# A hybrid encoder step: residual kept transposed, output projection with standing weights, the norm's factor applied after the projections

## Chip, cores and metric

One NeuronCore of a Trainium2 chip runs the whole program. The metric is the device time of one execution in microseconds (us), as a median over runs. The engines are named PE (TensorE), DVE (VectorE), ACT (ScalarE), POOL (GpSimd) and SP (SyncE, here the queue of all DMAs).

## What is computed

Four layers (A, B, C, A) update 576 tokens (512 of a prompt, 64 of a sample) of width 1024. Each layer has one input projection that gives the mixer's inputs and a gate of width 1024, a mixer, and an output projection:

```python
def rmsnorm(x, g):
    y = x * lax.rsqrt(jnp.mean(x * x, axis=-1, keepdims=True) + 1e-6)
    return y * g

def mixer_a(xp, ...):                       # chunked attention, 8 heads of 128
    z = rmsnorm(x, norm_g) @ w_in           # 1024 -> 4096: q, k, v, gate
    q, k = rmsnorm(q, q_g), rmsnorm(k, k_g) # per head
    o = band_attend(q, k, v, ...)
    return (o * silu(gate)) @ w_out         # 1024 -> 1024
# mixer_b: window attention, 16 query and 4 key heads of 64
# mixer_c: latent attention; q through a normed 512-wide latent, k and v through a normed 256-wide one
for i in range(4):
    x = x + mixer[i](x)
```

Besides the new x, the new keys, values and latents are outputs.

## The kernel before

All projections are f32 in two parts: each operand is split into a high part (rounded to fp32r by ACT, `AF.Copy`) and a low part (the difference, by DVE or POOL), and a product is three matmuls: high x high, high x low, low x high. They add up in one PSUM accumulator over the 8 blocks of 128 inputs. PSUM has three accumulators `mm` (`ps_mm`), two for transposes (`ps_t`), two for scores and one for attention outputs.

Activations for a projection stand transposed in SBUF, inputs on the partitions: `xT` (tile `T`) for the input projections, `oT` for the output projection. In `mm_tok` (lines 154 to 175) a tile of 128 tokens of these is the standing operand and up to 512 weight columns move; the last 64 tokens have their high and low parts side by side as one standing tile of 128, so they take two matmuls (lines 168 and 169) and a fold of the two halves (lines 172 to 174). In `gates` (line 211) the weights stand and half of the tokens, 288 columns, move (lines 224 to 226); the gate's tanh form is then multiplied into the branch result `o`.

The residual x lives in DRAM between layers, tokens on the rows. At the end of a layer `split_o` (line 250) splits each of the 8 blocks of the branch result into `oT`, high part on ACT, low part on POOL in two pieces (512 and 64 columns). `oT` lies in memory that the layer's own tiles have given up, and the blocks are interleaved with the last gates by `mix`. Then x is loaded again (`load_x`, 5 token tiles) and `out_proj` (line 256) runs over two halves of the output columns, each over 5 token tiles; after a tile's second half its x is stored and `norm` (line 184) makes the next layer's `xT` from it: a sum of squares on ACT, the factor per token by a power on POOL (`rstd`, line 112), two scaled copies on DVE (line 193), eight transposes on PE (line 178, `tr`), and the split out of PSUM (lines 181 and 182).

Weights are loaded in pieces of 256 KB (`load_chunk`: 512 columns of one block, `load_packed`: 256 columns of two blocks) into 4 staging buffers `ws` and split into 8 pairs `wh`, `wl`. Program order is that of the code; a planner then orders each engine's instructions by expected readiness before the launch, so that accumulators of one pool can be worked on side by side, and each engine runs its list in that order.

Of the kernel before, what the change touches and what calls it, by code (L numbers as in the profile page):

```python
# [18 lines left out]
D = 1024  # L19
# [21 lines left out]
def encoder_step(ctx: ExitStack, tc: tile.TileContext, I, O):  # L41
# [58 lines left out]
    x = []  # L100
# [3 lines left out]
    def load_x(pool, src):  # L104
        x.clear()
        for t, (t0, tn) in enumerate(TT):
            xt = sb(D, f"x{t}", pool=pool)
            last = ld(xt[:tn], src[t0 : t0 + tn, :])
            x.append(xt)
        return last.ins  # L110
# [43 lines left out]
    def mm_tok(xT, nh, t0, tn, pieces, n, p=None, c0=0, w0=0):  # L154
        p = p or ps_mm()
        last = len(pieces) - 1
        out = p[:, c0 : c0 + n]
        ws = slice(w0, w0 + n)
        for i, (h, l) in enumerate(pieces):
            if tn == 128:  # L160
                xh = xT[:, i, t0 : t0 + tn]
                xl = xT[:, i, nh + DEC + t0 : nh + DEC + t0 + tn]
                PE.matmul(out, xh, h[:, ws], start=(i == 0), stop=False)  # L163
                PE.matmul(out, xh, l[:, ws], start=False, stop=False)  # L164
                PE.matmul(out, xl, h[:, ws], start=False, stop=(i == last))  # L165
# [6 lines left out]
        lo = sb(512, "lo", 1)[:64, :n]  # L172
# [11 lines left out]
    def norm(t, g, xT):  # L184
        t0, tn = TT[t]
        ss = sb(1, "nss", pool=tiny)[:tn]
        junk = sb(D, "sq", 2, dt=BF16)[:tn]
        S.activation(junk, x[t][:tn], AF.Square, accum_out=ss)
        r = rstd(ss, tn, 1, 1.0 / D)
        for hf in range(2):  # L190
            xs = rows_of(tn)
            cs = slice(hf * 512, hf * 512 + 512)
            V.scalar_tensor_tensor(out=xs[:tn], in0=x[t][:tn, cs], scalar=r, in1=g[:tn, cs], op0=ALU.mult, op1=ALU.mult)  # L193
            pt = v3(ps_t(), 128)
            for j in range(4):
                tr(pt[:, j, :], xs[:, j * 128 : j * 128 + 128])
            k0 = hf * 4
            l0 = lo_at(t0, TOK)
            hl_evac(xT[:, k0 : k0 + 4, t0 : t0 + tn], xT[:, k0 : k0 + 4, l0 : l0 + tn], pt[:, :, :tn])
            if tn == DEC:  # L200
                end = V.tensor_copy(xT[:, k0 : k0 + 4, 2 * TOK : WT], xT[:, k0 : k0 + 4, TOK : TOK + DEC].bitcast(F32))
        return end.ins if tn == DEC else None
# [8 lines left out]
    def gates(xT, w, c0, ogs, done=None):  # L211
        st = []

        def half(m, og, hf):
# [12 lines left out]
            th = sb(512, "sq", 2)[:, :HALF]  # L227
# [22 lines left out]
    def split_o(oT, b, src):  # L250
        S.activation(oT[:, b, :TOK], src, AF.Copy)  # L251
        for a, c in ((0, SEQ), (SEQ, TOK)):
            l0 = lo_at(a, TOK)
            G.tensor_tensor(out=oT[:, b, l0 : l0 + c - a], in0=src[:, a:c], in1=oT[:, b, a:c].bitcast(F32), op=ALU.subtract)  # L254

    def out_proj(w, oT, after):
        for nh in range(2):
            pieces = load_chunk(w, [(nh * 512, 512)])
            for t in range(len(TT)):
                t0, tn = TT[t]  # L260
                p = mm_tok(oT, TOK, t0, tn, pieces, 512)
                xs = x[t][:tn, nh * 512 : nh * 512 + 512]
                V.tensor_tensor(out=xs, in0=p, in1=xs, op=ALU.add)  # L263
                after(t, nh)
# [7 lines left out]
    def layer_a(li, xT, first=None):  # L272
        w = I["a_w_in"][li]
        with tc.tile_pool(name=f"la{li}", bufs=1, reuse_waits="tile") as lp:
# [4 lines left out]
            def v_units(pr, pieces=None):  # L279
                st = [pieces] if pieces else []  # L280

                def unit(ts, tn):
# [11 lines left out]
                    S.activation(vt[:tn, ts[0] : ts[0] + n, :], v3(p, 256), AF.Copy)  # L294
                    for t in ts:
# [4 lines left out]
            def qk_units(pr):  # L300
                st = []

                def unit(t, t0, tn):
# [10 lines left out]
                    r = rstd(ss, tn, 4, 1.0 / 128)  # L314
# [131 lines left out]
    def layer_b(xT):  # L446
        w = I["b_w_in"][0]
        with tc.tile_pool(name="lb", bufs=1, reuse_waits="tile") as lp:
# [25 lines left out]
            for t, (t0, tn) in enumerate(TT):  # L474
# [27 lines left out]
            def q_units(g):  # L502
                w_ = []

                def unit(t, t0, tn):
# [9 lines left out]
                    r = rstd(ss, tn, 4, 1.0 / 64)  # L515
# [143 lines left out]
    def layer_c(xT):  # L659
        w = I["c_w_in"][0]  # L660
        with tc.tile_pool(name="lc", bufs=1, reuse_waits="tile") as lp:
# [52 lines left out]
            for t, (t0, tn) in enumerate(TT):  # L714
# [4 lines left out]
                r = rstd(ss, tn, 1, 1.0 / 512)  # L719
# [9 lines left out]
            for t, (t0, tn) in enumerate(TT):  # L729
# [5 lines left out]
                r = rstd(ss, tn, 2, [(0, 1, 1.0 / 256), (1, 2, 1.0 / 32)])  # L735
# [176 lines left out]
    def gain(pool, nm, i):  # L912
        g = sb(D, "gain", pool=pool)
        ld(g, I[f"{nm}_norm"][i : i + 1].to_broadcast([128, D]))
        return g

    layers = [("a", 0), ("b", 0), ("c", 0), ("a", 1)]
# [3 lines left out]
    with tc.tile_pool(name="xp0", bufs=1) as xp:  # L921
        for t, (t0, tn) in enumerate(TT):
            xt = sb(D, f"x{t}", pool=xp)
            ld(xt[:tn], I["x"][t0 : t0 + tn, :])
            x.append(xt)
            if t == 0:
                ld(ident, I["ident"])
                nxt_gain = gain(xp, "a", 0)
            if t < 4:
                src = I["a_w_in"][0][256 * t : 256 * t + 256, 2048:2304].rearrange("(a p) c -> p a c", p=128)  # L930
                h, l = load_w([src], 512, 256)
                first += [(h[:, 256 * i : 256 * i + 256], l[:, 256 * i : 256 * i + 256]) for i in range(2)]
            end = norm(t, nxt_gain, xT)
# [3 lines left out]
        with tc.issue_after(end):  # L937
            for a, b, f in ((0, 2, 128 ** -0.5), (2, 3, 64 ** -0.5), (8, 32, -1.0)):
# [3 lines left out]
    x_src = I["x"]  # L942
    for i, (kind, li) in enumerate(layers):
# [6 lines left out]
        x_new = dp.tile([TOK, D], F32, tag=f"xd{i}", name=f"xd{i}") if i < 3 else O["y"]  # L950
        nxt = {}

        def after(t, nh):
            t0, tn = TT[t]
            if i == 3:
                ld(x_new[t0 : t0 + tn, nh * 512 : nh * 512 + 512], x[t][:tn, nh * 512 : nh * 512 + 512])
            elif nh == 1:
                if "xT" not in nxt:
                    nxt["xT"] = big_xT()
                ld(x_new[t0 : t0 + tn], x[t][:tn])  # L960
                norm(t, nxt_gain, nxt["xT"])

        with tc.tile_pool(name=f"op{i}", bufs=1, reuse_waits="tile") as op:
            oT = v3(sb(KD * WT, "oT", dt=F32R, pool=op), WT)
# [3 lines left out]

            units = tail(put)
            after_gate = {"a": (6, 7), "b": (6, 7), "c": CT}[kind]  # L970
            mix([lambda b=b: put(b) for b in range(KD) if b not in after_gate], units)
            late[0] = load_x(op, x_src)
            if i < 3:
                nxt_gain = gain(op, *layers[i + 1])
            out_proj(I[f"{kind}_w_out"][li], oT, after)
# [5 lines left out]
    "y": (TOK, D),  # L981
# [94 lines left out]
```

## Time and profile before

| | |
|---|---|
| median of 3 runs | 1273.11 us (1271.35 to 1273.27) |
| the profiled execution | 1273.74 us, span of its instructions 1272.0 us |
| mean granted PE clock | 0.998 |
| PE, weight loads, DVE, ACT, POOL busy | 98%, 86%, 57%, 51%, 30% |
| DMA | 127.18 MB, mean 100 GB/s |

The span runs from the first to the last instruction of the program; launch and end lie around it. Matmuls are pipelined: the recorded duration of one overlaps the next, so the distance between starts, not the duration, is what a matmul costs in a stream.

### The profile page before, as it was taken

The numbers are of one execution on the slowest core, as the hardware profiler recorded it, in microseconds if no ns is written. First come the engines' busy times: TensorE is split into PE (matmuls) and PEld (weight loads), VectorE is DVE, ScalarE is ACT, GpSimd is POOL, SyncE is SP. The second block draws the span as 40 slices with busy tenths as digits, with TensorE's granted clock in tenths as the row PEclk, the third lists the DMA queues.
The fourth block names the chain that finished last, engine by engine and source line by source line (L and its number), as shares of the span: only waits on it lengthen the run. The fifth ranks groups of instructions, "written<-read, shape, count | busy, mean of one in ns | idle before, by whom it ended". The sixth has DMA issues, their size and how long they took to land.

```text
span 1272.0 us, 22132 instructions
## 1 busy us (share of the span) xinstructions
PE 1242.3 (98%) x7927; PEld 1090.7 (86%) x7927; DVE 719.3 (57%) x1979; ACT 647.7 (51%) x1645; POOL 383.1 (30%) x492
## 2 busy tenths in 40 slices
PE   5999999999999999999999999999999999999998
PEld 5889898998889999778998887876788898989986
DVE  5365535433668887526577767675264655354432
ACT  5345444553446776614466767676243454445431
POOL 5321212114035451331275444541311212121150
PEclk9999999999999999999999999999999999999999
DMA  7235241442446231344131111112343352414322
GB/s 210 83 96 152 77 140 53 141 128 76 154 126 215 74 87 51 113 121 137 57 101 53 53 30 34 34 51 69 98 157 99 94 159 73 144 43 138 129 80 70
DMA packets 99613, 127.18 MB, mean 100 GB/s; under 512 B 11184, under 2 KB 77648, under 8 KB 99440
## 3 DMA queue, kind: packets, MB, share of 16 engines
q1 hardware_dynamic: 99504, 125.77, 32.5%
q8 instruction: 62, 1.02, 0.3%
q14 instruction: 47, 0.39, 0.1%
HBM read 105.81 MB, written 24.26 MB: 102 GB/s over the span
## 4 chain that ended last, share of the span: by engine, by line
PE 94%; DVE 2%; ACT 2%; DMA 1%; issue 0%; POOL 0%; SPq 0%; DVEq 0%; POOLq 0%; ACTq 0%
PE mm L163 16%; PE mm L165 16%; PE mm L164 16%; PE t L178 9%; PE mm L224 5%; PE mm L225 5%; PE mm L226 5%; PE mm L168 4%; PE mm L169 4%; PE o L383 3%; PE s L858 3%; PE o L868 2%; PE s L375 2%; PE o L595 1%; PE s L562 1%; PE s L563 1%
## 5 line engine op out<-in xcount | busy, mean ns | idle before, releaser
L116 POOL TENSOR_TENSOR nv<-nv,mhalf 128x4 f32<-128x4 f32 (+7 forms) x147 | 150.9, 1031 | 470.8 <-DVE nv L115 446.7
L163 PE MATMUL mm<-wh,T 128*128 128x256 f32 (+2 forms) x736 | 246.3, 338 | 3.6 <-ACT T L181 2.4
L165 PE MATMUL mm<-wh,T 128*128 128x256 f32 (+2 forms) x736 | 246.4, 336 | 0.0
L164 PE MATMUL mm<-wl,T 128*128 128x256 f32 (+2 forms) x736 | 243.3, 335 | 0.0
L120 ACT ACTIVATE wh<-ws 128x512 fp32r<-128x512 f32 (+2 forms) x288 | 169.2, 614 | 111.9 <-PE mm L168 74.9
L121 DVE TENSOR_TENSOR wl<-ws,wh 128x512 fp32r<-128x512 f32 (+2 forms) x252 | 170.8, 698 | 48.2 <-ACT wh L120 44.7
L224 PE MATMUL mm<-T,wh 128*128 128x288 f32 x512 | 155.5, 304 | 0.1
L163 PEld LDWEIGHTS mm<-wh,T 128*128 128x128 f32 x736 | 140.8, 192 | 15.2 <-ACT T L181 2.8
L225 PE MATMUL mm<-T,wh 128*128 128x288 f32 x512 | 153.4, 300 | 0.0
L226 PE MATMUL mm<-T,wl 128*128 128x288 f32 x512 | 153.0, 299 | 0.0
L165 PEld LDWEIGHTS mm<-wh,T 128*128 128x128 f32 x736 | 140.7, 191 | 12.2 <-DVE T L182 0.2
L164 PEld LDWEIGHTS mm<-wl,T 128*128 128x128 f32 x736 | 140.4, 191 | 11.9
L232 POOL TENSOR_TENSOR o<-o,sq 128x288 f32<-128x288 f32 x52 | 43.9, 846 | 213.4 <-DVE sq L230 139.9
L163 PE MATMUL mm<-wh,oT 128*128 128x512 f32 x256 | 99.2, 396 | 2.5 <-ACT oT L251 1.9
L165 PE MATMUL mm<-wh,oT 128*128 128x512 f32 x256 | 99.7, 397 | 1.3 <-POOL oT L254 1.3
L164 PE MATMUL mm<-wl,oT 128*128 128x512 f32 x256 | 100.4, 395 | 0.0
L224 PEld LDWEIGHTS mm<-T,wh 128*128 128x128 f32 x512 | 96.2, 188 | 3.4 <-issue 1.9
L225 PEld LDWEIGHTS mm<-T,wh 128*128 128x128 f32 x512 | 96.2, 188 | 2.1 <-issue 1.8
L226 PEld LDWEIGHTS mm<-T,wl 128*128 128x128 f32 x512 | 96.2, 188 | 1.1 <-issue 1.1
L263 DVE TENSOR_TENSOR x<-mm,x 128x512 f32<-128x512 f32 x32 | 21.6, 689 | 117.3 <-PE mm L165 112.4
L178 PE MATMUL t<-ident,qs 128*128 128x128 f32 (+1 forms) x376 | 63.2, 280 | 13.1 <-DVE qs L193 7.5
L178 PEld LDWEIGHTS t<-ident,qs 128*128 128x128 f32 (+1 forms) x376 | 46.4, 141 | 21.9 <-DVE qs L193 7.2
(256 smaller groups left out, 2669.1 us busy)
## 6 DMA issues: line engine op xcount, KB each, us to landing
ws<-in_a_w_in SPq DMA_DIRECT2D x64, 256.0 KB, 3.1
ws<-in_a_w_in SPq DMA_DIRECT2D x128, 128.0 KB, 2.5
ws<-in_b_w_in SPq DMA_DIRECT2D x40, 256.0 KB, 3.0
ws<-in_a_w_out SPq DMA_DIRECT2D x32, 256.0 KB, 3.1
xd<-x SPq DMA_DIRECT2D x12, 512.0 KB, 2.6
x<-xd SPq DMA_DIRECT2D x12, 512.0 KB, 6.4
ws<-in_c_w_in SPq DMA_DIRECT2D x24, 256.0 KB, 3.1
out_akT<-kf SPq DMA_DIRECT2D x8, 576.0 KB, 3.6
```

Of the source, the lines that this page charges most:

```text
L116: G.tensor_tensor(out=r, in0=r, in1=bc(mhalf[:tn], tn, n), op=ALU.pow)
L120: S.activation(h, src, AF.Copy)
L121: (eng or G).tensor_tensor(out=l, in0=src, in1=h.bitcast(F32), op=ALU.subtract)
L163: PE.matmul(out, xh, h[:, ws], start=(i == 0), stop=False)
L164: PE.matmul(out, xh, l[:, ws], start=False, stop=False)
L165: PE.matmul(out, xl, h[:, ws], start=False, stop=(i == last))
L168: PE.matmul(out, xs, h[:, ws], start=(i == 0), stop=False)
L169: PE.matmul(out, xs, l[:, ws], start=False, stop=(i == last))
L178: PE.transpose(out, in_, perm or ident)
L224: PE.matmul(p, wh, xT[:, k, cs], start=(k == 0), stop=False)
L225: PE.matmul(p, wh, xT[:, k, ls], start=False, stop=False)
L226: PE.matmul(p, wl, xT[:, k, cs], start=False, stop=(k == KD - 1))
```

## The change

x is kept transposed (features on the rows) in DRAM and SBUF, in 8 blocks of 128 features by 576 tokens. The output projection lets weights stand and moves 288 tokens, as the gates do, so that its result is transposed like x. `feed` multiplies a block of x by the norm's gain alone and splits it into `xT`; the squares of a block are added to `acc`. `stats` sums `acc` over the partitions with five narrow matmuls, makes the factor per token `rr`, a copy `rb` of it on all partitions, and `ep`, the epsilon that stands for 1e-6 in a later norm of unscaled values. The factor then goes onto results: values get it when they leave PSUM (`scale=rr`), gates by a multiply with `rb`, and queries, keys and latents, which are normed again, get it through `ep` in `rstd`. The input x and the output y are transposed outside the device program.

```diff
     def load_x(pool, src):
...
+        for k in range(KD):
+            xk = sb(TOK, f"x{k}", pool=pool)
+            late[0] = ld(xk, src[128 * k : 128 * k + 128, :]).ins
-    def rstd(ss, tn, n, inv):
+    def rstd(ss, tn, n, inv, t=None):
+        e = EPS if t is None else ep[:tn, t : t + 1]
...
-            V.tensor_scalar(out=r[:, lo:hi], in0=ss[:, lo:hi], scalar1=f, scalar2=EPS, op0=ALU.mult, op1=ALU.add)
+            V.tensor_scalar(out=r[:, lo:hi], in0=ss[:, lo:hi], scalar1=f, scalar2=e, op0=ALU.mult, op1=ALU.add)
-    def norm(t, g, xT):
...
+    def feed(k, xk, g, xT, pool, eng, acc):
+        S.activation(xT[:, k, :TOK], xk, AF.Copy, scale=g[:, k : k + 1])
+        V.scalar_tensor_tensor(out=xT[:, k, TOK + DEC :], in0=xk, scalar=g[:, k : k + 1], in1=xT[:, k, :TOK].bitcast(F32),
+                               op0=ALU.mult, op1=ALU.subtract)
+        S.activation(xT[:, k, TOK : TOK + DEC], xT[:, k, 2 * TOK :].bitcast(F32), AF.Copy)
+        if k == 0:
+            S.activation(acc[:, :TOK], xk, AF.Square, scale=1.0 / 32)
+        else:
+            sq = sb(TOK, "xsq", 2, pool=pool)
+            S.activation(sq, xk, AF.Square, scale=1.0 / 32)
+            eng.tensor_tensor(out=acc[:, :TOK], in0=acc[:, :TOK], in1=sq, op=ALU.add)
+
+    def stats(pool, acc):
+        pt = ps_t()
+        for t in range(5):
+            PE.matmul(pt[:, 2 * t : 2 * t + 2], acc[:, 128 * t : 128 * t + 128], ones[:, 0:2], start=True, stop=True)
+        ve = sb(5, "ve", pool=tiny)
+        V.tensor_scalar(out=ve, in0=v3(pt[:, :10], 2)[:, :, 0], scalar1=EPS, scalar2=None, op0=ALU.add)
+        V.tensor_scalar(out=ep, in0=ve, scalar1=EPS, scalar2=None, op0=ALU.mult)
+        G.tensor_tensor(out=rr, in0=ve, in1=bc(mhalf, 128, 5), op=ALU.pow)
+        dg = v3(sb(5 * 128, "dg", pool=pool), 128)
+        for t in range(5):
+            end = V.tensor_scalar(out=dg[:, t, :], in0=ident, scalar1=rr[:, t : t + 1], scalar2=None, op0=ALU.mult)
+        for (a, b) in ((0, SEQ), (SEQ, TOK)):
+            pb = ps_t()[:, : b - a]
+            PE.matmul(pb, ones, dg.rearrange("p a b -> p (a b)")[:, a:b], start=True, stop=True)
+            S.activation(rb[:, a:b], pb, AF.Copy)
+        return end.ins
     def gates(xT, w, c0, ogs, done=None):
...
-            S.activation(th, p, AF.Tanh, scale=0.5)
+            V.tensor_tensor(out=z, in0=p, in1=rb[:, cs], op=ALU.mult)
+            S.activation(th, z, AF.Tanh, scale=0.5)
...
-            V.scalar_tensor_tensor(out=g, in0=th, scalar=1.0, in1=p, op0=ALU.add, op1=ALU.mult)
+            V.scalar_tensor_tensor(out=g, in0=th, scalar=1.0, in1=z, op0=ALU.add, op1=ALU.mult)
     def split_o(oT, b, src):
         S.activation(oT[:, b, :TOK], src, AF.Copy)
-        for a, c in ((0, SEQ), (SEQ, TOK)):
...
+        G.tensor_tensor(out=oT[:, b, TOK:], in0=src, in1=oT[:, b, :TOK].bitcast(F32), op=ALU.subtract)
-    def out_proj(w, oT, after):
...
+    def out_proj(w, oT, xs, after):
+        for pr in range(KD // 2):
+            pieces = load_packed(w, 256 * pr, 256)
+            for m in range(2):
+                db = 2 * pr + m
+                for hf in range(2):
+                    cs = slice(hf * HALF, hf * HALF + HALF)
+                    ls = slice(TOK + cs.start, TOK + cs.stop)
+                    p = ps_mm()[:, :HALF]
+                    for k, (h, l) in enumerate(pieces):
+                        wh = h[:, m * 128 : m * 128 + 128]
+                        wl = l[:, m * 128 : m * 128 + 128]
+                        PE.matmul(p, wh, oT[:, k, cs], start=(k == 0), stop=False)
+                        PE.matmul(p, wh, oT[:, k, ls], start=False, stop=False)
+                        PE.matmul(p, wl, oT[:, k, cs], start=False, stop=(k == KD - 1))
+                    V.tensor_tensor(out=xs[db][:, cs], in0=p, in1=xs[db][:, cs], op=ALU.add)
+                    after(db, hf)
...
+                        S.activation(vt[:tn, t, :], p[:, 256 * i : 256 * i + 256], AF.Copy, scale=rr[:tn, t : t + 1])
...
+        for k in range(KD):
+            ld(xk, I["xT"][128 * k : 128 * k + 128, :])
+            if k % 2 == 0:
...
+                h, l = load_w([src], 512, 256)
+            feed(k, xk, gains[0], xT, xp, V, acc)
+        ld(ident, I["ident"])
+        end = stats(xp, acc)
+        def after(db, hf):
...
+                ld(x_new[rows, cs], xs[db][:, cs])
+                feed(db, xs[db], gains[i + 1], nxt["xT"], op, G, acc)
+                ld(x_new[rows], xs[db])
...
+            xs = load_x(op, x_src)
+            out_proj(I[f"{kind}_w_out"][li], oT, xs, after)
             if i < 3:
+                stats(op, acc)
```

The fold's tile `lo` shares the buffer `hl` now, two small tiles of C's rotary embedding have one buffer instead of two, and the four gains are loaded as 128 x 8 tiles instead of rows spread over all partitions.

## Rows read from the trace of the kernel before

**Rows 1.** The page: engine busy time, share, instructions; shares of the chain that ended last.
```profile
PE 1242.3 (98%) x7927; PEld 1090.7 (86%) x7927; DVE 719.3 (57%) x1979; ACT 647.7 (51%) x1645; POOL 383.1 (30%) x492
...
PE 94%; DVE 2%; ACT 2%; DMA 1%; issue 0%; POOL 0%; SPq 0%; DVEq 0%; POOLq 0%; ACTq 0%
```

**Rows 2.** PE groups by line and shape: busy us, mean ns, idle before, what ended it.
```profile
L224 PE MATMUL mm<-T,wh 128*128 128x288 f32 x512 | 155.5, 304 | 0.1
...
L165 PE MATMUL mm<-wh,oT 128*128 128x512 f32 x256 | 99.7, 397 | 1.3 <-POOL oT L254 1.3
...
L178 PE MATMUL t<-ident,qs 128*128 128x128 f32 x312 | 53.6, 281 | 11.5 <-DVE qs L193 7.5 <-DVE T L182 2.9 <-DVE qs L517 0.9
...
L858 PE MATMUL s<-k,q 96*128 96x512 f32 x32 | 16.4, 609 | 0.0
```

**Rows 3.** PE timeline, second layer's output projection: start us, us, instruction.
```profile
544.73 0.39 PE L165 MATMUL mm<-wh,oT 128*128 128x512 f32 x1
...
551.50 0.40 PE L164 MATMUL mm<-wl,oT 128*128 128x512 f32 x1
```

**Rows 4.** PE timeline, a gate of the second layer.
```profile
533.07 0.29 PE L225 MATMUL mm<-T,wh 128*128 128x288 f32 x1
...
534.00 0.29 PE L226 MATMUL mm<-T,wl 128*128 128x288 f32 x1
```

**Rows 5.** The chain in order of time, a tile's transposes in the first boundary.
```profile
334.62 0.87 PE t L178 x8
```

**Rows 6.** Timeline of all engines, the end.
```profile
1266.73 0.59 ACT L173 ACTIVATE lo<-mm 64x512 f32<-64x512 f32 x1 [22.15 <-PE mm L169]
1267.36 0.68 DVE L174 TENSOR_TENSOR lo<-mm,lo 64x512 f32<-64x512 f32 x1 [3.67 <-ACT lo L173]
```

**Rows 7.** POOL timeline, split of the branch result before the first three projections.
```profile
300.50 1.57 POOL L254 TENSOR_TENSOR oT<-o,oT 128x512 fp32r<-128x512 f32 x2 [0.80 <-ACT oT L251]
...
537.12 10.72 POOL L254 TENSOR_TENSOR oT<-o,oT 128x512 fp32r<-128x512 f32 x14
547.79 0.80 POOL L232 TENSOR_TENSOR o<-o,sq 128x288 f32<-128x288 f32 x1
...
890.13 12.30 POOL L254 TENSOR_TENSOR oT<-o,oT 128x512 fp32r<-128x512 f32 x16
```

**Rows 8.** PE timeline in the same three places.
```profile
290.36 0.40 PE L163 MATMUL mm<-wh,oT 128*128 128x512 f32 x1
...
535.89 0.50 PE L163 MATMUL mm<-wh,oT 128*128 128x512 f32 x1 [1.01 <-ACT oT L251]
...
906.28 0.86 PE L165 MATMUL mm<-wh,oT 128*128 128x512 f32 x3
```

**Rows 9.** Groups by line and shape of DVE, ACT and POOL.
```profile
L230 DVE SCALAR_TENSOR_TENSOR sq<-sq,mm 128x288 f32<-128x288 f32 x52 | 23.4, 451 | 64.9 <-ACT sq L228 64.8
...
L251 ACT ACTIVATE oT<-o 128x576 fp32r<-128x576 f32 x32 | 19.6, 681 | 24.5 <-POOL o L232 24.5
...
L116 POOL TENSOR_TENSOR nv<-nv,mhalf 128x4 f32<-128x4 f32 x76 | 78.9, 1042 | 226.9 <-DVE nv L115 205.7 <-DVE ri L339 15.7 <-DVE ri L537 5.0
L121 POOL TENSOR_TENSOR wl<-ws,wh 128x512 fp32r<-128x512 f32 x36 | 46.1, 1298 | 16.4 <-ACT wh L120 14.8 <-PE t L178 0.8 <-DMA ws<-in_a_w_in 0.8
...
L254 POOL TENSOR_TENSOR oT<-o,oT 128x512 fp32r<-128x512 f32 x32 | 42.4, 1326 | 9.1 <-ACT oT L251 9.1
```

**Rows 10.** Waits: who for whom, total us, times, longest.
```profile
PE t L178 <- DVE qs L193: 7.5, 2, 7.2
```

**Rows 11.** Windows at the start: us, busy by engine, granted clock, DMA share, GB/s.
```profile
24.00:32.00 8.00, 5.06 (x31) 4.86 (x30) 5.36 (x5) 1.69 (x3) 2.86 (x5) 0.79 0.52 156
```

**Rows 12.** Timeline, the start: first use of x, first QK, last value matmul.
```profile
4.33 1.06 ACT L188 ACTIVATE sq<-x 128x1024 bf16<-128x1024 f32 x1 [2.32 <-DMA x<-in_x]
...
35.95 0.40 PE L163 MATMUL mm<-wh,T 128*128 128x512 f32 x1
...
39.30 0.28 PE L169 MATMUL mm<-wl,T 128*128 128x256 f32 x1
```

More of the change, by code (lines that the diff above doesn't have):

```diff
@@ L98, in rows_of @@
         return half[turn[0]]
-    x = []
+    ones = sb(128, "ones", pool=const)
+    V.memset(ones, 1.0)
+    rb = sb(TOK, "rb", pool=const)
+    rr = sb(5, "rr", pool=const)
+    ep = sb(5, "ep", pool=const)
     late = [None]
@@ L182, in hl_evac, with new_acc @@
         V.tensor_tensor(out=dst_l, in0=src, in1=dst_h.bitcast(F32), op=ALU.subtract)
-    def norm(t, g, xT):
[L185 to L202, printed above, removed]
+    def new_acc(pool):
+        acc = sb(5 * 128, "acc", pool=pool)
+        V.memset(acc[:, TOK:], 1.0)
+        return acc
@@ L910, in layer_c, with load_gain @@
         return og, lambda split: [u for b in CT for u in gate(b, done=lambda m: split(b))]
[L912 to L915, printed above, removed]
     layers = [("a", 0), ("b", 0), ("c", 0), ("a", 1)]
+    gains = []
+    for kind, li in layers:
+        gains.append(sb(KD, f"g{kind}{li}", pool=const))
+    def load_gain(i):
+        kind, li = layers[i]
+        ld(gains[i], I[f"{kind}_normT"][li])
     xT = big_xT()
@@ L921, in encoder_step @@
     with tc.tile_pool(name="xp0", bufs=1) as xp:
[L922 to L930, printed above, removed]
+        load_gain(0)
+        for k in range(KD):
+            xk = sb(TOK, f"x{k}", pool=xp)
+            ld(xk, I["xT"][128 * k : 128 * k + 128, :])
+            if k % 2 == 0:
+                src = I["a_w_in"][0][128 * k : 128 * k + 256, 2048:2304].rearrange("(a p) c -> p a c", p=128)
                 h, l = load_w([src], 512, 256)
                 first += [(h[:, 256 * i : 256 * i + 256], l[:, 256 * i : 256 * i + 256]) for i in range(2)]
-            end = norm(t, nxt_gain, xT)
+            if k == 0:
+                acc = new_acc(xp)
+            feed(k, xk, gains[0], xT, xp, V, acc)
+        ld(ident, I["ident"])
+        end = stats(xp, acc)
         ld(flip, I["flip"])
@@ L937, in encoder_step @@
         with tc.issue_after(end):
+            for i in range(1, 4):
+                load_gain(i)
             for a, b, f in ((0, 2, 128 ** -0.5), (2, 3, 64 ** -0.5), (8, 32, -1.0)):
@@ L949, in encoder_step @@
             ogs, tail = layer_c(xT)
-        x_new = dp.tile([TOK, D], F32, tag=f"xd{i}", name=f"xd{i}") if i < 3 else O["y"]
+        x_new = dp.tile([D, TOK], F32, tag=f"xd{i}", name=f"xd{i}") if i < 3 else O["yT"]
         nxt = {}
[L953 to L961, printed above, removed]
         with tc.tile_pool(name=f"op{i}", bufs=1, reuse_waits="tile") as op:
-            oT = v3(sb(KD * WT, "oT", dt=F32R, pool=op), WT)
+            oT = v3(sb(KD * 2 * TOK, "oT", dt=F32R, pool=op), 2 * TOK)
+            if i < 3:
+                acc = new_acc(op)
             def put(b):
                 split_o(oT, b, ogs[b])
+            def after(db, hf):
+                rows = slice(128 * db, 128 * db + 128)
+                if i == 3:
+                    cs = slice(hf * HALF, hf * HALF + HALF)
+                    ld(x_new[rows, cs], xs[db][:, cs])
+                elif hf == 1:
+                    if "xT" not in nxt:
+                        nxt["xT"] = big_xT()
+                    feed(db, xs[db], gains[i + 1], nxt["xT"], op, G, acc)
+                    ld(x_new[rows], xs[db])
             units = tail(put)
@@ L1059 @@
     out = (
[L1060 to L1061 removed]
+        r["yT"].T[None, :SEQ],
+        r["yT"].T[None, SEQ:],
         akT[:, None, :SEQ],
```

59 lines of the change are left out of this document (22 added, 37 removed).

## Prediction

> **What bounds the kernel now.** I read the page's engine table first: TensorE (PE) is busy 98% of the 1272.0 us span and carries 94% of the chain that ended last [rows 1]. A busy PE is not by itself a PE at its rate, so I went to the spacing of the matmuls in the timeline. In the output projection 30 matmuls of 512 columns start between 544.73 and 551.50, one per 0.233 us, without a gap [rows 3]; in the gates 8 matmuls of 288 columns start between 533.07 and 534.00, one per 0.133 us [rows 4]. The groups by shape give mean durations of 397 ns for 512 columns and 304 ns for 288 [rows 2], 0.17 us more than the spacing: the tail of one lies under the next. So PE issues at its rate almost everywhere, and a matmul taken away is time taken away, if what feeds PE keeps up. The places where it does not keep up now are the start and the beginning of an output projection; they decide the rest.
>
> **Output projection, matmuls.** Before, a layer needs 2 halves x (4 token tiles x 8 x 3 + 8 x 2) = 224 matmuls of 512 columns: 224 x 0.233 = 52.2 us. After, 8 blocks x 2 halves x 8 x 3 = 384 of 288 columns. The nearest rows are the gates, which have the same shape and the same roles (weights standing, activations moving), so I take their 0.133: 384 x 0.133 = 51.1 us. Gain 1.1 us a layer, 4.6 in all. Bounds: in proportion to the columns it would be 0.233 x 288 / 512 = 0.131, a gain of 7.6. On the other side, the spacing of 0.233 is 20 ns over 512 columns at 2.4 columns per ns; the gates' 0.133 is 13 ns over. If the 20 ns belong to the output projection's tile and not to its shape, a matmul takes 0.140, 53.8 us a layer, a loss of 6.2 in all.
>
> A rule speaks against the edit. The Trainium skill (TensorE: Matmul & The Clock Gate, section Back-to-back issue gap) says that in a stream with a weight load per matmul, 512 columns take about 131 ns and 128 columns about 81 ns, so a narrow matmul costs more per column. Between these, 288 columns would be an estimate of 102 ns, and a layer 384 x 0.102 = 39.2 against 224 x 0.131 = 29.3 us, 9.8 us more; four layers would cost 39 us in place of the gain and the kernel would end near 1305. The trace differs at both ends (0.233 and 0.133), with a price nearly in proportion to the columns, so the sum goes by the trace; what the trace leaves open of it is rival (d).
>
> **The norm's transposes.** A boundary has 5 tiles x 8 transposes. A tile's 8 stand in the chain with 0.87 us, 0.109 each, among projection matmuls that wait behind them [rows 5]. 40 x 0.109 = 4.4 us a boundary, 13.2 for the three; the first norm's 40 are counted with the start.
>
> **The statistics.** New on PE are, per norm, five matmuls of 2 columns and two broadcasts of 512 and 64 columns in plain f32. A 128-column f32 transpose lasts 281 ns, or 0.11 of spacing; a 512-column f32 matmul lasts 609 [rows 2], less the 0.17 tail 0.44. So 5 x 0.11 + 0.44 + 0.11 = 1.1 us, 3.3 for three boundaries. Bounds: 0.6 (the narrow ones nearly free) to 2.
>
> **The output projection's beginning.** Here a cover goes away. The branch result is split for the projection by ScalarE (ACT, high part) and GpSimd (POOL, low part), one block of 128 inputs after another, and POOL is the slow one: after the third layer's attention 16 pieces, 8 blocks, take 12.30 us from 890.13; after the second 7 blocks take 10.72 from 537.12, then a gate product at 547.79 and one block more; after the first the last block ends at 302.07 [rows 7]. Meanwhile PE works ahead in three open accumulators: the three last matmuls of such a set begin at 906.28, 16.2 us after POOL's row, and PE shows no wait on POOL in it [rows 8]. A set is 72 matmuls x 0.233 = 16.8 us, longer than POOL needs. After, three accumulators hold 72 x 0.133 = 9.6 us. POOL has one piece of 576 columns for two: between 1.33 (the 512 piece alone [rows 9]) and 1.53 (10.72 / 7), I take 1.42, about the middle. So:
> - third layer: last low part at 890.13 + 8 x 1.42 = 901.5, the set ends 0.4 later, 12.0 us after its start instead of 9.6: 2.4 us of new idle time.
> - second layer: POOL is done at 537.1 + 7 x 1.42, then 0.8, 0.7 and 1.42, 550.0, and the set 0.4 later. PE starts it at 535.89 [rows 8] and already loses 1.3 to POOL [rows 2]; with 9.6 of work it would be done at 546.8: 3.6 new.
> - first and fourth layer: the projection starts at 290.36 [rows 8], a set of 9.6 would end at 300.0, the last low part is ready at 302.07 less 8 x 0.11, 301.2: 1.2 each.
> Together +8.4. Bounds: 4, if the order on POOL is rearranged, and 14, if the gates' longer chain (below) delays the last block too.
>
> **The boundary.** The next layer's input block 7 is ready only when the last group is added (0.45 us, the nearest DVE row), copied by ACT (0.68) and subtracted by DVE (0.7-0.8) [rows 9]: some 2.4 us. The next projection has 21 matmuls on blocks 0 to 6 in each of three accumulators before it needs block 7, at least 21 x 0.12 = 2.5 us. Covered. The statistics follow later: a square on ACT, a sum on POOL (1.42), PE, a power on POOL (1.04 [rows 9]), PE again. If PE's order puts one of these matmuls a little early, PE waits; the old chain of the same kind cost PE 7.5 us in two waits, 7.2 of them at the start [rows 10]. I take 1 us per boundary, +3, with bounds 0 and 15.
> Loads and stores: x comes and goes in 8 tiles instead of 5 and the four broadcast gains go; about 6 more issues a boundary of some 0.45 us on SyncE's queue, with the weight loads queued behind the stores. The weights need 4 loads per 12.8 us and half the weight buffers are a whole block ahead, so I cost them at nothing; without that lead a late load (3 us) would show whole.
>
> **The gates** take one DVE multiply more per half, 64 x 0.45 = 29 us on an engine 57% busy [rows 1]. PE's accumulator is free earlier, so it costs only where a gate result is last before the projection or DVE is full (second layer): +1, bounds 0 and 4. Halving the values' copy and the smaller buffers go under the same cover: nothing.
>
> **The start.** PE does 5.06 of 8 us between 24 and 32 at a mean granted clock of 0.79 [rows 11]; its first QK matmul starts at 35.95 and the last value matmul at 39.30 [rows 12]. By 39.4 it has delivered 112 value matmuls (13.4 us) and 11 QK matmuls (2.6): 23.4 us are lost. After, no work waits for a per-token norm; ACT sets the pace: per block two passes of 0.68, one narrow pass of some 0.25, and half a weight split of 0.62, 1.9 us, from about 4.3 [rows 12] to 19.7. If PE follows block by block in its three accumulators (1.68 us a block), the values end near 22 and the QK weights, split on POOL at 1.3 us each [rows 9], allow the first QK group near 28, 18.8 us of work done: 9.2 lost, a gain of 14. If it takes the token tiles in turn, nothing but the first tile is done at 20 and the gain is 2. I take 9: half the way, and a little more because the planner interleaves accumulators elsewhere [rows 8].
>
> **The tail.** The last sample tile's fold, 0.59 on ACT and 0.68 on DVE [rows 6], goes, the add narrows by 0.24, and one hand-over of 0.1 is saved: -1.6.
>
> **Sum.** -4.6 - 13.2 + 3.3 + 8.4 + 3 + 1 - 9 - 1.6 = -12.7 on the profiled execution's 1273.74: 1261.0. (Its span is 1272.0; 1.7 lie around it.) That execution stands 0.6 above the median of the runs, too little to move the figure.
>
> **Rivals.**
> (a) The feeding is hidden (0.20): the split keeps up, no boundary wait, the start gains all 14. -4.6 - 13.2 + 3.3 + 4 - 14 - 1.6 = -26.1, 1248. For it: the planner's interleaving; against: POOL's durations.
> (b) The feeding takes most of it back (0.12): the projections' beginnings cost 12, the boundaries 4, and the start gives 4: -4.6 - 13.2 + 3.3 + 12 + 4 + 1 - 4 - 1.6 = -3.1, 1271. For it: POOL's rows; against: PE's reordering.
> (c) Slower (0.08): PE's queue holds the statistics ahead of the next layer's matmuls. Then each boundary pays the chain whole: 0.45 + 0.68 + 0.68 + 1.42 + 0.7 + 0.4 + 1.04 + 5 x 0.45 + 0.7 and ten hand-overs of 0.1 (an estimate from the gaps between such rows), 9.3 us; three are 27.9 in place of 3, 1286. It decides from 5.2 us a boundary on. For it: PE runs its queue in order. Against: rows 10.
> (d) The narrow matmul carries a fixed 20 ns as the wide one does (0.05): 0.140 in place of 0.133, 1536 x 0.007 = +10.8, 1272, no change. For it: rows 3; against: rows 4.
>
> **How the numbers follow.** The forecast holds 0.55 with its own range of 1253 to 1267. The range of 8 in 10 takes in (a) and most of (b): 1246 to 1270. A difference of 0.2% (2.5 us) is about what can be told from none: faster 0.85, same 0.07, slower 0.08.
>
> **What would show it.** Spacing in the new projection near 0.133; L178 gone from the boundaries; PE waiting on the split's POOL line for 2 to 5 us in layers two and three; the first QK matmul before 30. Wrong would be a wait of PE on the statistics, or a start that still fills 35 us.

## The result, and the profile after

The changed kernel takes 1286.65 us (median of 4 runs, 1285.53 to 1288.88), the kernel before beside it 1272.51 (1271.35 to 1273.27): a ratio of 1.0116, 95% interval 1.0102 to 1.0129. It is slower by some 14 us; the forecast was 1261.0, with a range of 1246 to 1270.

The page of the changed kernel, engine table and chain, against [rows 1]:

```profile
span 1284.6 us, 23327 instructions
...
PE 1241.3 (97%) x8463; PEld 1126.0 (88%) x8463; DVE 737.8 (57%) x2023; ACT 662.1 (52%) x1677; POOL 401.3 (31%) x465
...
PE 89%; DVE 3%; POOL 2%; issue 2%; DMA 1%; ACT 1%; SPq 0%; POOLq 0%; DVEq 0%; ACTq 0%
```

Subtract PE's busy time from the span. Before, 1272.0 - 1242.3 = 29.7 us without a matmul; after, 1284.6 - 1241.3 = 43.3. The idle time grew by 13.6 and the busy time shrank by only 1.0, though whole groups of transposes are gone. Both numbers want an explanation: where PE waits, and why less work does not take less time.

Line numbers are from here on those of each run's own kernel. In the changed kernel L169 to L175 are the input projections' matmuls, L179 and L180 the fold, L184 the transposes, L197 and L205 VectorE's part of `feed`, L210 to L221 `stats`, L249 to L254 a gate, L273 and L274 the branch result's split, L288 to L290 the output projection, L126 and L127 the weights' split. The waits, who for whom, total us, times, longest:

```profile
PE mm L169 <- ACT wh L126: 7.6, 1, 7.6
PE mm L288 <- DVE sq L249: 4.9, 3, 2.2
PE mm L169 <- DVE hl L180: 4.6, 2, 2.9
PE t L220 <- DVE dg L217: 3.6, 1, 3.6
PE mm L171 <- DVE T L197: 2.6, 3, 2.2
PE mm L288 <- ACT oT L273: 2.4, 3, 1.1
PE mm L289 <- POOL oT L274: 2.3, 3, 1.0
PE t L184 <- DVE nv L121: 1.8, 1, 1.8
...
PE t L184 <- ACT v L506: 1.2, 1, 1.2
```

The first is the wait for the first input and weights, about as long before. The others of this list are in the main four stories.

*The start.* PE's timeline: the statistics, the broadcast of the factor, the first QK matmul.

```profile
27.83 1.18 PE L210 MATMUL t<-ones,acc 128*128 128x2 f32 x10
...
35.27 2.05 PE L220 MATMUL t<-dg,ones 128*128 128x512 f32 x4 [3.64 <-DVE dg L217]
37.08 0.78 PE L169 MATMUL mm<-wh,T 128*128 128x512 f32 x1
```

The last value matmul starts at 31.35 where it started at 39.30 before [rows 12], as hoped; but the broadcast L220 stands in PE's queue ahead of QK and waits 3.64 us. QK begins at 37.08, later than before. Each f32 product is also two instructions: ten for five products, four for two. What L220 waits for is slow itself: VectorE's five products L217 take 4.16 us, beside three of GpSimd's weight splits. At the first boundary, where no such split runs, five take 1.08 (357.71); at that pace 0.6 of the 3.64 us would be left.

```profile
31.12 4.16 DVE L217 TENSOR_SCALAR dg<-ident,rr 128x128 f32<-128x128 f32 x5 [1.14 <-POOL rr L214]
```
```profile
31.05 3.71 POOL L127 TENSOR_TENSOR wl<-ws,wh 128x512 fp32r<-128x512 f32 x3
```

*The second layer's fold.* ACT's copy for the last sample tile, then PE:

```profile
385.00 0.59 ACT L179 ACTIVATE hl<-mm 64x512 f32<-64x512 f32 x1 [2.94 <-DMA out_bkT<-hl]
```
```profile
386.45 0.36 PE L169 MATMUL mm<-wh,T 128*128 128x256 f32 x1 [2.94 <-DVE hl L180]
...
387.24 0.41 PE L169 MATMUL mm<-wh,T 128*128 128x256 f32 x1
387.45 0.42 PE L170 MATMUL mm<-wl,T 128*128 128x256 f32 x1
```

The fold now shares its buffer with the keys that are being sent out, waits until they have left, and PE waits with it. And then: 0.8 us after PE resumes, the spacing of 256 columns goes from 0.12 to 0.21 us, which is 1.2 columns per ns, the lower of TensorE's two clock levels.

*The statistics at a boundary.* ACT holds copies in order; L221 copies the broadcast:

```profile
364.04 0.71 ACT L221 ACTIVATE rb<-t 128x512 f32<-128x512 f32 x2 [4.78 <-PE t L220]
...
365.15 0.84 ACT L506 ACTIVATE v<-mm,rr 128x256 f32<-128x256 f32 x2
```

For 4.78 us ACT empties no accumulator, and PE stands for 1.25 us (L184 <- ACT v L506), in the third layer for 1.75 (L184 <- DVE nv L121, behind ACT's copy L221 there too); at the third boundary it does not stand.

*The last gate before the first projection*, on VectorE and, in the second fence, GpSimd:

```profile
289.16 3.00 DVE L252 SCALAR_TENSOR_TENSOR sq<-sq 128x288 f32<-128x288 f32 x2
292.08 6.17 DVE L127 TENSOR_TENSOR wl<-ws,wh 128x512 fp32r<-128x512 f32 x4
298.17 0.45 DVE L249 TENSOR_TENSOR sq<-mm,rb 128x288 f32<-128x288 f32 x1
```
```profile
286.01 9.28 POOL L274 TENSOR_TENSOR oT<-o,oT 128x576 fp32r<-128x576 f32 x6 [2.82 <-ACT oT L273]
295.25 2.45 POOL L254 TENSOR_TENSOR o<-o,sq 128x288 f32<-128x288 f32 x2
```

L252 takes 1.5 us each; before, with one operand in PSUM, it took 0.45 [rows 9]. The queue behind it is late, the accumulator of the last gate is read only at 298.17, and PE, which has run out of open accumulators, waits 2.23 us.

Why less work took as long shows in windows of 8 us (busy us of PE, PEld, DVE, ACT, POOL; granted clock; DMA share; GB/s):

```profile
296.00:304.00 8.00, 5.77 (x33) 5.54 (x32) 3.26 (x4) 1.81 (x3) 5.74 (x5) 0.79 0.37 106
...
384.00:392.00 8.00, 5.55 (x34) 5.58 (x35) 3.95 (x12) 2.92 (x8) 2.99 (x4) 0.79 0.31 85
392.00:400.00 8.00, 8.00 (x69) 8.00 (x68) 6.46 (x22) 6.06 (x17) 5.21 (x5) 1.00 0.15 42
...
544.00:552.00 8.00, 7.68 (x45) 7.49 (x45) 0.50 (x1) 2.20 (x5) 8.00 (x7) 0.79 0.64 225
```

The window behind the fold's wait holds 34 matmuls in 5.55 us of busy time, the next one 69 in 8. Ten windows of the changed kernel have a mean clock under 0.98, before it was one ahead of the tail [rows 11]. It does not follow every wait: the same wait of 2.23 us stands at 1232.06, and the matmuls behind it keep their 0.133.

```profile
1234.29 0.40 PE L288 MATMUL mm<-oT,wh 128*128 128x288 f32 x1 [2.23 <-DVE sq L249]
...
1234.93 0.29 PE L289 MATMUL mm<-oT,wh 128*128 128x288 f32 x1
1235.06 0.30 PE L290 MATMUL mm<-oT,wl 128*128 128x288 f32 x1
```

But on the whole a wait is paid nearly twice: once idle (13.6 us), once in matmuls at the lower level (the 12.6 that the busy time lacks: with all four edits of the experiments it is 13.6 below before and not 1.0). An estimate from the windows agrees: what their granted clock lacks to 1, times 8 us, is 13.5 us in sum after and 2.2 before.

### The profile page after: what moved, and what is told of

Read it like the earlier page. It is cut to its first block, busy times and chain, and to the rows that moved or that the text cites. A ratio compares the mean times of both kernels' runs of the same rounds, so it can differ in the third digit from the quotient of the medians.

```text
span 1284.6 us, 23327 instructions
## 1 busy us (share of the span) xinstructions
PE 1241.3 (97%) x8463; PEld 1126.0 (88%) x8463; DVE 737.8 (57%) x2023; ACT 662.1 (52%) x1677; POOL 401.3 (31%) x465
## 4 chain that ended last, share of the span: by engine, by line
PE 89%; DVE 3%; POOL 2%; issue 2%; DMA 1%; ACT 1%; SPq 0%; POOLq 0%; DVEq 0%; ACTq 0%
PE mm L169 11%; PE mm L171 11%; PE mm L170 11%; PE t L184 7%; PE mm L244 5%; PE mm L245 5%; PE mm L246 5%; PE mm L289 5%; PE mm L288 5%; PE mm L290 5%; PE o L411 3%; PE s L886 3%; PE mm L174 2%; PE mm L175 2%; PE s L403 2%
## 5 line engine op out<-in xcount | busy, mean ns | idle before, releaser
L169 PE MATMUL mm<-wh,T 128*128 128x256 f32 (+2 forms) x736 | 247.3, 339 | 11.4 <-ACT wh L126 7.6
L122 POOL TENSOR_TENSOR nv<-nv,mhalf 128x4 f32<-128x4 f32 (+6 forms) x127 | 137.3, 1086 | 321.1 <-DVE nv L121 282.2
L126 ACT ACTIVATE wh<-ws 128x512 fp32r<-128x512 f32 (+2 forms) x288 | 170.6, 616 | 72.7 <-PE mm L289 32.8
L127 DVE TENSOR_TENSOR wl<-ws,wh 128x512 fp32r<-128x512 f32 (+2 forms) x252 | 176.4, 714 | 53.2 <-ACT wh L126 41.3
L169 PEld LDWEIGHTS mm<-wh,T 128*128 128x128 f32 x736 | 141.4, 193 | 23.0 <-ACT wh L126 7.6
L288 PE MATMUL mm<-oT,wh 128*128 128x288 f32 x512 | 152.0, 302 | 7.4 <-DVE sq L249 4.9
L289 PE MATMUL mm<-oT,wh 128*128 128x288 f32 x512 | 153.9, 302 | 2.4 <-POOL oT L274 2.3
L245 PE MATMUL mm<-T,wh 128*128 128x288 f32 x512 | 153.4, 300 | 0.0
L290 PE MATMUL mm<-oT,wl 128*128 128x288 f32 x512 | 153.1, 300 | 0.0
L254 POOL TENSOR_TENSOR o<-o,sq 128x288 f32<-128x288 f32 x52 | 43.6, 840 | 207.4 <-DVE sq L252 133.5
L288 PEld LDWEIGHTS mm<-oT,wh 128*128 128x128 f32 x512 | 97.8, 193 | 9.6 <-DVE sq L249 5.6
L289 PEld LDWEIGHTS mm<-oT,wh 128*128 128x128 f32 x512 | 98.6, 193 | 3.8 <-POOL oT L274 3.8
L290 PEld LDWEIGHTS mm<-oT,wl 128*128 128x128 f32 x512 | 98.8, 193 | 0.0
L245 PEld LDWEIGHTS mm<-T,wh 128*128 128x128 f32 x512 | 96.3, 188 | 1.7 <-issue 1.5
```

The source lines that it names most:

```text
L126: S.activation(h, src, AF.Copy)
L127: (eng or G).tensor_tensor(out=l, in0=src, in1=h.bitcast(F32), op=ALU.subtract)
L245: PE.matmul(p, wh, xT[:, k, ls], start=False, stop=False)
L288: PE.matmul(p, wh, oT[:, k, cs], start=(k == 0), stop=False)
L289: PE.matmul(p, wh, oT[:, k, ls], start=False, stop=False)
L290: PE.matmul(p, wl, oT[:, k, cs], start=False, stop=(k == KD - 1))
```

## Experiments

Theory W: the time went into new waits of PE, many with a stretch at the lower clock behind them. Theory O: the new order and contention in general, so that a wait taken away comes back elsewhere. Idle is the span less PE's busy time, each from the kernel's page, which shows one execution (for buffer + broadcast the fastest, 1273.08); the ratio is to runs of the kernel before on the same chip; differences in the text are of medians.

| kernel | median us | range | ratio (95%) | idle | busy |
|---|---|---|---|---|---|
| before | 1272.51 | 1271.35-1273.27 | | 29.7 | 1242.3 |
| changed | 1286.65 | 1285.53-1288.88 | 1.0116 (1.0102-1.0129) | 43.3 | 1241.3 |
| own fold buffer | 1280.96 | 1279.56-1283.54 | 1.0060 (1.0043-1.0077) | 41.1 | 1238.1 |
| broadcast later | 1290.17 | 1288.95-1292.08 | 1.0132 (1.0115-1.0150) | 46.8 | 1243.4 |
| gate in PSUM | 1281.94 | 1280.61-1283.45 | 1.0067 (1.0050-1.0084) | 43.2 | 1237.0 |
| five accumulators | 1273.61 | 1270.98-1275.45 | 1.0004 (0.9993-1.0016) | 36.6 | 1236.1 |
| buffer + broadcast | 1278.17 | 1273.08-1279.39 | 1.0038 (1.0024-1.0051) | 36.1 | 1235.1 |
| buffer + gate + five | 1264.29 | 1261.95-1271.10 | 0.9943 (0.9923-0.9963) | 32.9 | 1228.0 |
| the same, broadcast later at the start | 1264.91 | 1263.41-1265.67 | 0.9936 (0.9925-0.9947) | 31.4 | 1230.2 |
| all four | 1259.07 | 1257.45-1260.50 | 0.9891 (0.9876-0.9906) | 29.9 | 1228.7 |
| all four, squares on PE | 1266.03 | 1265.40-1267.63 | 0.9943 (0.9931-0.9956) | 21.1 | 1244.8 |
| all four, start's splits on DVE | 1257.38 | 1255.79-1258.59 | 0.9882 (0.9865-0.9898) | 26.5 | 1229.4 |
| before, shared buffer | 1278.76 | 1277.61-1281.64 | 1.0053 (1.0039-1.0068) | 31.8 | 1244.0 |
| before, five accumulators | 1270.47 | 1268.32-1273.59 | 0.9976 (0.9966-0.9987) | 26.5 | 1241.1 |

**Own fold buffer.**
```diff
-                    st = v3(sb(512, "hl", 1), 128)[:64, :, :tn]
+                    st = v3(sb(512, "bst", 1, pool=lp), 128)[:64, :, :tn]
...
-            cst = v3(sb(512, "hl", 1), 256)
+            cst = v3(sb(512, "ex", 4), 256)
```


> The changed kernel with the fold tile's buffer no longer shared with the second layer's key tile that is sent out and the third layer's cache load: these two get buffers of their own. Theory W (new waits of TensorE, each followed by a stretch at the lower clock): the waits on L180 of 2.94 us at 383.5 and 1.69 us at 665.9 go, and the clock loss behind the first, so 1286.7 falls by 5 to 8 us, to 1279-1282. Theory O (the planner's new order and contention in general; a wait taken away comes back at the next place): within 2 us of 1286.7.

5.7 us gained, as theory W has it; no wait on L180 is left. PE's idle time falls by 2.2 where these waits had 4.6, so some of it came back at other lines.

**The kernel before with that sharing alone** (its fold tile's tag `lo` becomes `hl`).

> The kernel before with the one memory saving of the change alone: its fold tile shares the buffer of the second layer's sent-out key tile and the third layer's cache load. Theory W: the waits of 2.9 and 1.7 us that the changed kernel shows on L180 appear in the kernel before too, with the clock loss behind the longer one: 4 to 8 us slower than before, 1277-1281. Theory O, or the wait hidden by the older order: within 2 us of 1272.9.

6.4 us lost, where nothing of the change but the memory saving was made. PE's wait there:
```profile
PE mm L163 <- DVE hl L174: 4.4, 1, 4.4
```

**Five accumulators in the output projection.**
```diff
-                    p = ps_mm()[:, :HALF]
+                    p = (ps_s if (2 * db + hf) % 5 > 2 else ps_mm)()[:, :HALF]
```


> The changed kernel with the output projection taking its accumulators in turn from three matmul banks and the two banks of the attention's scores, so that TensorE can work ahead in five groups, 72 + 48 matmuls or 16.0 us, as long as in the kernel before. Theory W (the split's cover was lost): the idle time at the beginning of the second and third layer's projections, 3.3 and 1.9 us, goes with the clock loss behind it, 5 to 9 us in all, 1278-1282. Rival (TensorE takes the groups in turn and does not work ahead, or the banks are still held by the attention): within 2 us of 1286.7.

13.0 us gained, more than W's upper bound, because the first and fourth layers' waits for the gate went too: PE had other groups to go on with. The same window as above, then the second layer's:
```profile
296.00:304.00 8.00, 8.00 (x62) 8.00 (x61) 5.27 (x7) 3.38 (x6) 6.25 (x5) 1.00 0.41 124
...
544.00:552.00 8.00, 8.00 (x60) 8.00 (x59) 2.58 (x2) 1.95 (x3) 7.20 (x7) 0.96 0.28 74
```
62 matmuls in place of 33. Idle time falls by 6.7 and busy time by 5.2, the two payments of a wait.

**The kernel before with five accumulators.**

> The kernel before with five accumulators in its output projection instead of three. It has 3.3 us of idle time at the beginnings of its projections. If the five accumulators repair only the cover that the change took away: within 2 us of 1272.4. If they are an improvement of their own, worth as much in either kernel: 1264-1268.

3.2 us of its own (1273.67 beside it), against 13.0 in the changed kernel: between the two bounds, so in the changed kernel mostly a repair of the cover. PE's waits for `oT` fall only from 3.2 to 2.8 us here; the rest came at other places in the new order.

**Gate in PSUM.**
```diff
-            zt = v3(sb(TOK, "sq", 2), HALF)
-            z, th = zt[:, 0, :], zt[:, 1, :]
+            z, th = p, sb(512, "sq", 2)[:, :HALF]
```


> The changed kernel with the gate's factored input written back into the accumulator instead of SBUF, so that the last gate operation reads one SBUF operand as in the kernel before, and the accumulator is held through tanh as before. Theory W (two SBUF operands on VectorE beside GpSimd's split are what delays the last gate and the weight's low parts ahead of the first and fourth output projection): L252 falls from up to 1.5 us each to near 0.5, the waits of 2.2 us at 296 and 1232 halve, 2 to 5 us gained, 1282-1285. Rival (the accumulators held longer cost as much as is gained, or GpSimd's own split sets the end): 1285-1289.

4.7 us gained. VectorE at the same place, and PE's first two waits there:
```profile
288.88 0.82 DVE L251 SCALAR_TENSOR_TENSOR sq<-sq,mm 128x288 f32<-128x288 f32 x2 [0.22 <-ACT sq L249]
289.71 4.41 DVE L127 TENSOR_TENSOR wl<-ws,wh 128x512 fp32r<-128x512 f32 x3
294.05 0.45 DVE L248 TENSOR_TENSOR mm<-mm,rb 128x288 f32<-128x288 f32 x1
```
```profile
297.39 0.54 PE L287 MATMUL mm<-oT,wh 128*128 128x288 f32 x2 [1.11 <-ACT oT L272]
...
298.24 0.40 PE L287 MATMUL mm<-oT,wh 128*128 128x288 f32 x1 [0.32 <-DVE sq L251]
```
With one operand in PSUM two gate operations take 0.82 us in place of 3.00, beside the same GpSimd split, while the weight splits (two SBUF operands) stay at 1.5 each. PE waits 1.4 us in two pieces for 2.23 in one; idle time hardly fell (43.2), busy time did, by 4.3, and the granted clock of the window 296 to 304 is 1.00 in place of 0.79.

**Broadcast later.** `stats` ends with the factor per token; the rest becomes a function called behind the first QK or Q units, or the third layer's KV latent.
```diff
+    def spread():
+        dg = sb(TOK, "sq", 2)
+        for t, (t0, tn) in enumerate(TT):
+            V.tensor_scalar(out=dg[:, t0 : t0 + tn], in0=ident[:, :tn], scalar1=rr[:, t : t + 1], scalar2=None, op0=ALU.mult)
...
             run(u[1:])
+            spread()
```


> The changed kernel with the broadcast of the norm's factor (five products with the identity, two matmuls with ones, two copies) issued later: in the first and fourth layer behind the first group of QK units, in the second behind the first Q units, in the third behind the KV latent. The factor per token for the values stays where it is. Theory W: at the start TensorE's wait of 3.64 us for the products goes and QK begins near 32 in place of 37.1; at the boundaries ScalarE no longer holds the accumulators: the waits of 1.25 us at 365.4 and 1.75 us at 619.4 shrink, with the clock loss behind them; together 6 to 10 us, 1277-1281. Theory O: the start's gain is met again at the first attention; less than 2 us.

3.5 us lost. The waits it aimed at are gone, but two others came: 5.5 us on the shared fold buffer in the third layer, and this in the second (VectorE; GpSimd; PE):
```profile
431.48 4.89 DVE L605 TENSOR_SCALAR ex<-ex,ri 128x128 f32<-128x128 f32 x4
```
```profile
431.34 4.95 POOL L127 TENSOR_TENSOR wl<-ws,wh 128x512 fp32r<-128x512 f32 x4
```
```profile
437.35 0.58 PE L592 MATMUL s<-k,q 128*128 128x256 f32 x1 [5.10 <-DVE nm L598]
```
Four small products take 4.89 us (0.87 at 404.66 in the changed kernel), just as long as GpSimd's four splits. The Trainium skill (SBUF — State Buffer, section SBUF: two separate sides) says that VectorE and GpSimd share a pair of ports which one instruction holds whole: GpSimd's, or VectorE's if it has two SBUF inputs or runs in a two-port mode. The trace agrees in the durations here and at L252 above (1.5 us in place of 0.45); whether the four products run in such a mode, no row shows.

**Buffer and broadcast.**

> The changed kernel with two of the four edits: the fold tile's buffer not shared and the broadcast later. The fold's buffer alone gave 1281.0, the later broadcast alone 1290.2. If the later broadcast lost only by meeting the shared buffer and a clash of VectorE with GpSimd: 1275-1279. If a later broadcast costs in itself: 1283 or more.

1278.17, inside the first bound and 2.8 below the buffer alone, with intervals that overlap. The later broadcast shows no cost of its own; its loss was in what it met.

**Three edits; the same with the broadcast later at the start; all four.**

> The changed kernel with three edits together: the fold tile's buffer not shared, the gate's factored input back in the accumulator, five accumulators for the output projection. Theory W: the separate waits add up, the gate's edit except, since with five accumulators nothing waits for the last gate any more: 1286.7 - 13.0 - 5.7 = 1268.0, with up to 2 more from the gate; 1265-1269, below the kernel before. Theory O (a wait taken away comes back elsewhere as the order changes): 1271-1277.

> The three edits together and, at the start alone, the broadcast of the norm's factor issued behind the first QK group; at the three boundaries it stays where the changed kernel has it. Theory W: the first layer's main stage shortens by the 2.8 us that the run with the later broadcast showed there, up to 5, against the run of the three edits; 1261-1266. Theory O: no difference to the three edits.

> The three edits together and the broadcast issued later everywhere. If the loss of the run with the later broadcast alone (1290.2) came from the shared fold tile in the third layer (a wait of 5.5 us at 668) and from one clash of VectorE with GpSimd's weight split in the second (4.9 us for four products at 431.5), the first goes with the tile's own buffer and the second goes or stays by chance of the order: 1258-1268. If a later broadcast is itself the cost: 3 us or more above the run with the broadcast late at the start alone.

Three edits give 1264.29, 22.4 below the changed kernel and 0.7 below W's range; the separate gains are 23.4, so by the medians they add up. By the ratios it is 22.0 of 27.6 us, and the gate's edit beside the other two is worth 3.6 us by the medians and 0.6 by the ratios. With some 2 to 3 us of uncertainty on each gain (an estimate from the intervals) it is not established that the gate's edit keeps its worth there. Later at the start alone gave nothing: the first projection begins 2.0 us earlier (288.2 for 290.2), but in the third layer PE now waits 3.2 us for a gate (L245 <- DVE o L252), a miss for W and what O says. Later everywhere gave 5.2 more: 1259.07. PE's idle time is then what it was before the change, 29.9 us, and its busy time is 13.6 lower.

**Squares summed by PE at the start** (on all four).
```diff
+        for t, (t0, tn) in enumerate(TT):
+            PE.matmul(pt[:tn, 2 * t : 2 * t + 2], sq[:, t0 : t0 + tn], ones[:, 0:2], start=False, stop=False)
```


> The four edits together, and at the start the squares are summed by TensorE (five matmuls of 2 columns a block into one accumulator, as the blocks come) instead of by seven adds on VectorE, each of which reads two SBUF operands. Theory D (VectorE, slowed by GpSimd's weight splits beside it, paces the start: 8.0 us busy of 8 between 16 and 24): its adds, some 0.7 to 1.8 us each, go, the value projection ends 3 to 6 us earlier and the run falls to 1253-1257. Rival T (the loads or ScalarE pace it, or the clock's loss stays): within 2 us of 1259.1.

7.0 us lost: the experiment tells nothing on VectorE, because PE itself became the bound.
```profile
14.24 6.21 PE L199 MATMUL t<-ones,xsq 128*128 128x2 f32 x30
...
30.89 0.41 PE L171 MATMUL mm<-wh,T 128*128 128x256 f32 x1
31.11 0.41 PE L169 MATMUL mm<-wh,T 128*128 128x256 f32 x1
```
A matmul of 2 columns takes 0.2 us here, and PE, which from 7.10 on has no gap, still does 256 columns in 0.21 us at 31. That is the lower level, though the granted clock reads 1.00 in these windows; at the start of a trace the spacing tells the level.

**The start's weight splits on VectorE** (on all four).
```diff
-    weng[0] = G
+    weng[0] = V
     with tc.tile_pool(name="xp0", bufs=1) as xp:
```


> The four edits together, and in the start, up to the first group of QK units, the weights' low parts are split by VectorE instead of GpSimd, so that no GpSimd operation reads SBUF beside VectorE's feeding. Theory D (VectorE's operations with two SBUF operands are held up by GpSimd's there: 1.8 us in place of 0.8, seven times or so): the feeding takes 8 x 0.81 + 7 x 0.75 + 4 x 0.69 = 14.5 us from 6.7 in place of 16.3, no operation of it takes over 1 us, the last block is ready near 21 in place of 23.1 and the run gains 1.5 to 4 us, 1255-1257.5. Rival (VectorE has as much to do in sum, and what follows the last block sets the start): within 1 us of 1259.1.

1257.38, 1.7 below all four, on another chip (ratios 0.9882 and 0.9891, whose intervals overlap: the gain in the total is not established). The stage shows the mechanism. VectorE's last feeding operations, changed kernel first, this one second:
```profile
18.88 1.84 DVE L205 TENSOR_TENSOR acc<-acc,xsq 128x576 f32<-128x576 f32 x1
20.64 1.82 DVE L197 SCALAR_TENSOR_TENSOR T<-x,ga,T 128x576 fp32r<-128x576 f32 x1
```
```profile
18.09 0.81 DVE L197 SCALAR_TENSOR_TENSOR T<-x,ga,T 128x576 fp32r<-128x576 f32 x1
18.82 0.75 DVE L205 TENSOR_TENSOR acc<-acc,xsq 128x576 f32<-128x576 f32 x1
```
No feeding operation takes over 0.82, the last block is ready at 18.9 in place of 22.5 (all four: 23.1), QK begins at 29.76 (35.11), and the first projection at 286.0 (289.7). 1.6 us are lost again in the second projection (54.3 us from its first matmul to its last, 52.7 with all four).

## Why the prediction was wrong

- **Matmul work: right.** PE's busy time in the kernel with all four edits is 13.6 us below before, with equal idle time; the sum had -4.6 - 13.2 + 3.3 = -14.5. That they meet so closely is in part luck. The busy time also holds the first norm, which the forecast put with the start, and the statistics were mis-sized: 1.0 + 1.0 us a norm in place of 1.1, two instructions for each f32 product. With four norms at these prices the sum is -4.6 - 17.6 + 8.0 = -14.2. The spacing in the new projection is 0.133 (51.1 us for 384), not the 0.140 of rival (d). It is not the price either that the Trainium skill (TensorE: Matmul & The Clock Gate, Back-to-back issue gap) gives, by the prediction's estimate 0.102.
- **"The smaller buffers go under the same cover: nothing"** is the step that failed outright. The one shared by the fold cost 5.7 us in the changed kernel and 6.4 in the kernel before. The prediction put it at nothing without asking who holds the buffer: a DMA on its way out. (The other saving, C's two rotary tiles, is written and read by GpSimd alone, in order, so no other engine waits for that buffer; no run took it back.)
- **The projection's beginning, +8.4, was seen and mis-sized.** PE's idle time there is 4.9 + 2.4 + 2.3 = 9.6 us (L288 and L289 in the waits above) where it was 3.2: 6.4 new. That this is near 8.4 is luck, since it stands in other places. The first and fourth layers lose 2.2 each and not 1.2, to the gate's chain on VectorE, which the forecast bounded but did not price. The second and third lose 0.9 and 1.0 more than before and not 3.6 and 2.4, and PE's waits for GpSimd's split come to 1.3 and 1.0 there, where 2 to 5 had been announced: much of the time went into matmuls at the lower clock (45 in the window from 544, 60 with five accumulators). Five accumulators gave back 13.0, against 3 in the kernel before: the lower clock behind the waits stands in no term of the sum.
- **"The gates +1"** counted VectorE's multiply as 0.45 us and not what the last operation becomes with both operands in SBUF beside GpSimd: 4.7 us by the experiment, and beside the other two edits 3.6 by the medians (1273.6 - 5.7 - 1264.3) or 0.6 by the ratios, so not established there.
- **The boundary, +3: about right** in idle time (1.25 + 1.75, none at the third). Rival (c) named the mechanism, PE's queue holding statistics ahead of the next matmuls, and placed it wrongly: 3.64 at the start, under 2 at a boundary, and there by way of ACT. Its 1286 is the time that was measured, but by luck: it charged 9.3 us to each of three boundaries. Later broadcasts are worth 2.8 to 5.2 us once the buffer is free.
- **The start, -9, did not come:** first projection at 291.5 after, 290.4 before; the prediction's own sign of being wrong, a start that still fills 35 us, is there. VectorE and not ACT set the pace (last block 22.5, not 19.7; ACT had its high part done at 17.3, though its first pass began at 5.65, behind a table load of 1.28 us that in the kernel before ran at 0.72, ahead of x). And PE did not follow with 14 matmuls a block: it had two of the four full token tiles open beside the sample, so that 54 of the 112 value matmuls were still to do when the last block came, and the last of them started at 31.35 where the forecast had the values done near 22. Some ran at half rate, 0.21 us each from 9.3 to 11.6 and from 22.9 to 25.2.
- **The tail: right**, 3.6 us from the last matmul to the end in place of 5.7, -2.1 for -1.6.

So the loss of 14.1 us is a gain of about that size, undone by waits that are paid nearly twice (some 3 us of the five accumulators' worth, which the kernel before gets too, are no part of the change). Taken apart, by medians, the edits give 13.0 + 5.7 + 4.7 and 2.8 to 5.2, 26 to 29; together they gave 27.6. What stays open: how the start's missing 9 us divide between VectorE's pace, the order of the value matmuls and the clock (the last run has 4.4 of them), and a wait of 3.1 us on L180 at 647 in the third layer with all four edits, where VectorE has copies of 2.1 us queued ahead (an order to try, not tried). A planner orders the whole kernel anew at each edit, so single differences under 3 us may be its doing.

## What to carry to other kernels

Price an edit's memory savings like its instructions: for each buffer that gets a second user, ask who holds it longest, and a DMA on its way out counts until it has landed. Narrower work units shrink the cover that open accumulators give, so count the work they hold against the slowest producer and add accumulators in the same edit. On a kernel that keeps TensorE busy, price a wait of 1 to 3 us at its length and up to twice that.

## What the runs showed of the hardware

- Behind waits of 1 to 3 us matmuls often, not always, ran at half rate for some us: 0.21 us for 256 columns behind 2.94 us at 383.5, granted clock 0.79 in the window behind 2.23 us at 296.4, full rate behind 2.23 us at 1232.1.
- VectorE operations next to GpSimd ones stretched from 0.82 to 1.8 us, four small products from 0.87 to 4.89, five from 1.08 to 4.16; the same gate operation with one operand in PSUM kept its 0.41 to 0.45.
- A plain f32 matmul is two instructions; with 2 columns each takes 0.1 us at the higher clock level (ten in 1.03) and 0.2 at the lower, as the spacing of 256 columns around it tells it (thirty in 6.14).
